# Attention layer: TensorE, VectorE and ScalarE run in a written order, probabilities are turned two units and multiplied four units behind their scores

## The chip, the cores and the metric

The kernel runs on one core of one Trainium2 chip. The metric is the device time of one execution in microseconds (us); a time that is reported is the median over runs. TensorE (PE) does matmuls and transposes, VectorE (DVE) and ScalarE (ACT) read and write PSUM and SBUF, GpSimd (POOL) works on SBUF, and SyncE (SP) issues most DMAs. Products that need fp32 accuracy are made of three single-pass products: each operand is split into a high part (rounded, `hi`) and a remainder (`lo`), and hi·hi + hi·lo + lo·hi is accumulated. In the code this is the loop over `PASS`.

## The reference, cut to what matters

A model of two layers works on 512 latent tokens and 256 context tokens of width 1024. Layer 0 is a gated DeltaNet and isn't touched. Layer 1 is attention with 8 query heads on 2 key/value heads of width 128, for the latent rows only:

```python
def gqa_attend(q, k, v):
    qg = q.reshape(b, lq, 2, 4, 128)
    s = jnp.einsum('bqhgd,bkhd->bhgqk', qg, k).astype(F32) * (d ** -0.5)
    p = jax.nn.softmax(s, axis=-1).astype(v.dtype)
    return jnp.einsum('bhgqk,bkhd->bqhgd', p, v).reshape(b, lq, hq, d)

# layer 1
u_lat, u_ctx = modulated_rms_norm(h_lat), modulated_rms_norm(h_ctx)
q, k, v, z = split(u @ w_in, [1024, 256, 256, 1024])   # q, k: RMS norm per head, then axial rotary
y_lat = (gqa_attend(q, concat(k_ctx, k_lat), concat(v_ctx, v_lat)) * silu(z)) @ w_out
out   = rms_norm(h_lat + gate * y_lat)
```

## The kernel before, in words

Line numbers are those of the kernel before, as in its profile. Layer 1 fills the last 334 us of the span, from about 985 us. The order in which each engine takes its instructions is set there by a scheduler that works when the program is built: it takes the program's order and a cost for each instruction, and puts independent work into gaps it sees. (Layer 0 has one loop, at L1045, whose order is written out by hand instead.) A buffer that is used again makes the new writer wait for the last user of the old contents.

**Inputs.** `u_block(k)` turns 128 columns of the residual stream into the transposed, modulated input `uL`: matmuls with a diagonal matrix into a PSUM bank (L1159), DVE scales and shifts it (L1161), ACT writes hi (L1162), DVE lo (L1163). `kv_block(k)` accumulates k and v (L1225). `kv_norm` takes sums of squares on ACT (L1233) and calls `rsqrt`. `k_tile(t)` rotates keys (L1256 and L1257 on DVE, an add on POOL, L1258) and `to_T` transposes them (PE L1264, ACT L1266 hi, DVE L1267 lo).

**Two shared PSUM banks.** `ptr` (L1069) is a pool of two PSUM banks with the tag `tr`. They are used in turn by `u_block`, by every `to_T`, by each half of every `turn`, and by `room` (L1088), which lends a bank as scratch to `rsqrt`. With `room`, `rsqrt` is a chain of 15 DVE operations on 128x8 (L163 to L172), most of them with one operand in PSUM; without it, 12 operations that have all operands in SBUF (L163, L164, L174 to L179).

**Units.** There are 32 units u: query head hq = u // 4, block of 128 rows t = u % 4. For a unit, `scores` makes 128x768 scores in `s3[:, u % 2]`: three matmuls on the 512 columns of the half's own bank (L1348), three on the 256 columns of the bank that both halves share (L1351). DVE takes the row maximum (L1353) and multiplies it by the query's norm factor r (L1355), ACT takes the exponential with its row sum (L1358), DVE the reciprocal (L1359), ACT scales the rows (L1360). `turn` transposes the 768 columns in two groups of three (PE L1373), each followed by ACT hi (L1375) and DVE lo (L1376). `values`, once per two units, does 18 matmuls into `po` (L1385); DVE multiplies by the gate z (L1387), ACT and POOL split the result (L1389, L1390).

**Pieces.** While units run, PE also projects z and q for the later heads. A `z_piece` is half of one head's z, 12 matmuls of 512 columns (L1335), with tanh (L1338) and a DVE product (L1339) behind the second half. A `q_piece` is 24 matmuls of 256 columns (L1319), two squares on ACT (L1322), the rotation on DVE (L1249 once, L1252 twice), an add on POOL (L1253), `to_T`, and behind t = 3 `rsqrt`. Eight units form a period that starts at u0 = 8p: z at u0 and u0+1, q for t = 0 to 3 at u0+2 to u0+5, z at u0+6 and u0+7. Each new q or z weight is cast and split on POOL (L1194, L1195). In the last period six `out_block` calls (6 matmuls of 512 columns each, L1404) take the place of pieces; the output weights are split on POOL (L1440, L1441).

The loop that says the program's order is short:

```python
    for u in range(32 + 3):
        if u < 32:
            scores(u)
        if u in pieces1:
            f_, x, y = pieces1[u]
            f_(x, y)
        if 0 <= u - 1 < 32:
            turn(u - 1)
        if u >= 3 and u % 2:
            values((u - 3) // 2)
```

Of the kernel before, what the change touches and what calls it, by code (L numbers as in the profile page):

```python
# [86 lines left out]
def backbone(tc, a, out):  # L87
# [1222 lines left out]
    def q_piece(p, t):  # L1310
# [4 lines left out]
        wq, sq = qTs["w", p], qTs["s", p]  # L1315
        pgq = pg[1 - t // 2].rearrange("p (t n) -> p t n", t=2)
        for k in range(KT):
            for n_, (i, j) in enumerate(PASS):
                T.matmul(pgq[:, t % 2], uL[i][:, k, t * P:(t + 1) * P], wq[j][:, k], start=k == 0 and n_ == 0, stop=k == KT - 1 and n_ == 2)  # L1319
        for h in range(2):  # L1320
            jk = tmp.tile([P, P], F32, tag="jk", name=f"qj{p}{t}{h}")
            S.activation(jk, pgq[:, t % 2, h * P:(h + 1) * P], AF.Square, accum_out=sq[:, t, h:h + 1])  # L1322
# [5 lines left out]
    def z_piece(hq, half):  # L1328
# [4 lines left out]
        for k in range(half * 4, half * 4 + 4):  # L1333
            for n_, (i, j) in enumerate(PASS):
                T.matmul(pg[b], wz[j][:, k], uL[i][:, k], start=k == 0 and n_ == 0, stop=k == KT - 1 and n_ == 2)  # L1335
        if half == 1:
            zt = at.tile([P, NLAT], F32, tag="zt", name=f"zt{hq}", bufs=3)
            S.activation(zt, pg[b], AF.Tanh, scale=0.5)  # L1338
            V.scalar_tensor_tensor(zt, zt, 1.0, pg[b], ALU.add, ALU.mult)  # L1339
            zts[hq] = zt  # L1340

    def scores(u):
# [3 lines left out]
        for n_, (i, j) in enumerate(PASS):  # L1346
            q = qTs[hq // 2][i][:, hq % 2, t * P:(t + 1) * P]
            T.matmul(s3[:, b, own], q, kT[j][:, g, own], start=n_ == 0, stop=n_ == 2)  # L1348
        for n_, (i, j) in enumerate(PASS):
            q = qTs[hq // 2][i][:, hq % 2, t * P:(t + 1) * P]  # L1350
            T.matmul(s3[:, b, shared], q, kT[j][:, g, shared], start=n_ == 0, stop=n_ == 2)  # L1351
# [1 line left out]
        V.tensor_reduce(nm_, s3[:, b], AX.X, ALU.max, negate=True)  # L1353
# [1 line left out]
        V.tensor_tensor(nm_, nm_, r, ALU.mult)  # L1355
# [2 lines left out]
        S.activation(pr, s3[:, b], AF.Exp, bias=nm_, scale=r, accum_out=sm)  # L1358
# [19 lines left out]
    def values(u2):  # L1378
# [4 lines left out]
        for kt_ in range(NT):  # L1383
            for n_, (i, j) in enumerate(PASS):
                T.matmul(po, vv[i][:, kt_, g * P:(g + 1) * P], pT[j][:, kt_], start=kt_ == 0 and n_ == 0, stop=kt_ == NT - 1 and n_ == 2)  # L1385
# [125 lines left out]
```

## Time and profile before

| | |
|---|---|
| runs | 1324.54 us median of 3 (1322.84, 1324.54, 1326.51) |
| profiled execution | span 1319.2 us from the first to the last instruction; the profile gives no other time of its own |
| busy over the span | PE 1182.4 us (90%), DVE 840.3 (64%), ACT 708.9 (54%), POOL 640.2 (49%) |
| chain of work that ended last | PE 51%, DVE 13%, POOL 11%, DMA 10%, ACT 9% |
| layer 1, from 985 us | PE 286.5 us busy of 334.2 |

A row of the timeline gives the start, the time until the end of the last of a run of equal instructions, engine, line, operation, output and inputs, and in brackets the idle time of the engine ahead of it and what ended it. A row of the table by windows gives start, end, length, then the busy time of PE, its weight loads, DVE, ACT and POOL, the granted clock of TensorE (1 is full speed), the share of the DMA engines and GB/s. A row of the groups gives busy time and the mean of one in ns. Starts of rows are 985 us and more because layer 0 comes first.

### The profile page before, as it was taken

To read this page: it belongs to the slowest core of one execution; us is meant where nothing else is said; L and a number is where in the kernel's file an instruction comes from. 1 tells how busy PE (TensorE), PEld (TensorE's weight loads), DVE (VectorE), ACT (ScalarE), POOL (GpSimd) and SP (SyncE) were. 2 spreads that over 40 slices of the span, in tenths; PEclk is the share of its full clock that TensorE was granted. 3 is DMA by queue.
4 is the path that set the end of the run, shared out by engine and by line. 5 is a ranking of instruction groups with operands and counts; after the bars stand their busy time and mean duration, and the time that the engine had idled before them with its cause. 6 is when DMAs were issued, how large, how long until landed. Compare 5 with 4: busy or idle time off the path is not lost.

```text
span 1319.2 us, 28137 instructions
## 1 busy us (share of the span) xinstructions
PE 1182.4 (90%) x10803; PEld 946.5 (72%) x10803; DVE 840.3 (64%) x1784; ACT 708.9 (54%) x1892; POOL 640.2 (49%) x503
## 2 busy tenths in 40 slices
PE   3999999998889798999988897897999879998886
PEld 1676778887778687886555565775777669887674
DVE  3688567768796456866767775654355567655635
ACT  3343336764666789856877774533332234565531
POOL 0121142079999998004754785575663144322520
PEclk9999999999899899999999999998999899998988
DMA  8367975464455796559999897544542021101113
GB/s 316 133 210 224 334 223 154 139 174 140 125 165 150 191 277 214 182 182 262 220 215 213 205 223 177 182 154 128 187 146 65 1 64 49 48 1 65 64 64 96
DMA packets 235304, 209.81 MB, mean 159 GB/s; under 512 B 51073, under 2 KB 195618, under 8 KB 234274
## 3 DMA queue, kind: packets, MB, share of 16 engines
q1 hardware_dynamic: 216354, 198.58, 52.2%
q10 hardware_dynamic: 18816, 9.44, 2.5%
q8 instruction: 85, 1.39, 0.5%
q14 instruction: 49, 0.40, 0.1%
HBM read 167.21 MB, written 40.67 MB: 158 GB/s over the span
## 4 chain that ended last, share of the span: by engine, by line
PE 51%; DVE 13%; POOL 11%; DMA 10%; ACT 9%; issue 4%; SPq 2%; ACTq 0%; DVEq 0%; POOLq 0%
PE ks L963 5%; PE g_q L324 5%; PE g_z L324 4%; PE po L1123 4%; DMA cT<-t_d 3%; POOL X L664 3%; PE pg L1319 3%; PE g_k L324 3%; PE kv L1225 3%; PE po L1385 3%; PE su L1019 3%; POOL tmp L663 2%; POOL wol L859 2%; PE pg L1335 2%; PE pr L989 2%
## 5 line engine op out<-in xcount | busy, mean ns | idle before, releaser
L972 POOL TENSOR_TENSOR S<-S,glb 128x512 f32<-128x512 f32 x88 | 89.9, 1042 | 128.4 <-DMA cv<-v_d 70.4
L1123 PE MATMUL po<-woh,y 128*128 128x512 f32 x384 | 128.1, 404 | 12.3 <-ACT y L887 9.1
L859 POOL TENSOR_TENSOR wol<-wo,woh 128x1024 fp32r<-128x1024 f32 x32 | 76.5, 2396 | 54.4 <-ACT woh L858 46.9
L324 PE MATMUL g_v<-uh,wh 128*128 128x512 f32 (+1 forms) x256 | 90.4, 353 | 11.6 <-DVE sil_v L350 11.6
L664 POOL TENSOR_TENSOR X<-X,tmp 128x62 f32<-128x62 f32 (+15 forms) x93 | 96.8, 1041 | 6.7
L963 PE MATMUL ks<-S,ckq 128*64 128x256 f32 x768 | 96.1, 392 | 0.6 <-ACT O L969 0.6
L324 PE MATMUL g_z<-uh,wh 128*128 128x512 f32 (+1 forms) x256 | 88.9, 347 | 7.8 <-DVE sil_v L350 7.8
L1123 PEld LDWEIGHTS po<-woh,y 128*128 128x128 f32 x384 | 71.9, 192 | 28.7 <-ACT y L887 9.8
L663 POOL TENSOR_TENSOR tmp<-L,X 128x62 f32<-128x62 f32 (+15 forms) x93 | 88.0, 946 | 6.7
L324 PE MATMUL g_v<-ul,wh 128*128 128x512 f32 (+1 forms) x256 | 89.3, 349 | 0.0
L324 PE MATMUL g_v<-uh,wl 128*128 128x512 f32 (+1 forms) x256 | 88.6, 346 | 0.0
L324 PE MATMUL g_z<-uh,wl 128*128 128x512 f32 (+1 forms) x256 | 87.4, 341 | 0.0
L324 PE MATMUL g_z<-ul,wh 128*128 128x512 f32 (+1 forms) x256 | 87.3, 341 | 0.0
L346 DVE SCALAR_TENSOR_TENSOR acc_v<-g_v,cwv,acc_v 128x510 f32<-128x510 f32 (+3 forms) x128 | 75.7, 610 | 17.4 <-ACT acc_v L343 15.4
L963 PEld LDWEIGHTS ks<-S,ckq 128*64 128x64 f32 x768 | 52.0, 139 | 41.9 <-ACT O L969 7.1
L1123 PE MATMUL po<-wol,y 128*128 128x512 f32 x192 | 78.5, 409 | 3.4 <-POOL wol L859 3.4
L306 POOL TENSOR_TENSOR wl_k<-w_k,wh_k 128x1024 fp32r<-128x1024 f32 x8 | 19.0, 2380 | 101.8 <-ACT wh_k L305 101.8
L324 PEld LDWEIGHTS g_v<-uh,wh 128*128 128x128 f32 x256 | 50.3, 196 | 18.1 <-DVE sil_v L350 12.1
L1037 DVE TENSOR_TENSOR S<-su,S 128x512 f32<-128x512 f32 x88 | 56.6, 685 | 7.2 <-PE su L1019 6.1
L966 DVE SCALAR_TENSOR_TENSOR r<-ks,negV,cv 128x128 f32<-128x128 f32 x192 | 56.4, 344 | 4.9 <-PE ks L963 3.8
L324 PEld LDWEIGHTS g_z<-uh,wh 128*128 128x128 f32 x256 | 49.3, 193 | 13.8 <-DVE sil_v L350 8.6
L1022 DVE TENSOR_TENSOR O<-pq,O 128x512 f32<-128x512 f32 x48 | 33.2, 691 | 40.5 <-PE pq L1011 35.3
(372 smaller groups left out, 3435.1 us busy)
## 6 DMA issues: line engine op xcount, KB each, us to landing
aw<-in_ada_w SPq DMA_DIRECT2D x24, 1024.0 KB, 7.7
w<-in_dn_w_in SPq DMA_DIRECT2D x40, 512.0 KB, 4.6
wo<-in_dn_w_out SPq DMA_DIRECT2D x32, 512.0 KB, 3.2
cv<-v_d SPq DMA_DIRECT2D x96, 128.0 KB, 3.5
df<-gc_d SPq DMA_DIRECT2D x48, 128.0 KB, 2.8
z_d<-zs SPq DMA_DIRECT2D x16, 384.0 KB, 4.7
v_d<-vt ACTq DMA_DIRECT2D x16, 384.0 KB, 4.4
t_d<-Tt SPq DMA_DIRECT2D x6, 1024.0 KB, 4.1
```

Source lines behind the costliest of these rows:

```text
L324: mm = T.matmul(pg_[:m, :n], w[:, k, :m], u[:, k, c0:c0 + n], start=k == 0 and n_ == 0, stop=k == KT - 1 and n_ == 2)
L346: V.scalar_tensor_tensor(acc[:, c0 + lo:c0 + hi], ps[:, lo + j - 2:hi + j - 2], cwv[:, j, ct:ct + 1], acc[:, c0 + lo:c0 + hi], ALU.mult, A ...
L663: E.tensor_tensor(tv, bcast(L[:, :, j + 1:, j], 3, j + 1), bcast(X[:, :, j, 0:j + 1], 2, n), ALU.mult)
L664: E.tensor_tensor(X[:, :, j + 1:, 0:j + 1], X[:, :, j + 1:, 0:j + 1], tv, ALU.subtract)
L859: G.tensor_tensor(wl, w, wh, ALU.subtract)
L963: T.matmul(ks[r0:r0 + 64, w], kq[:, hh, w, r0:r0 + 64], St[hh][:, d], start=True, stop=True)
L966: V.scalar_tensor_tensor(r[:, 2 * j + i], ks[:, 0, i], negV[:, visit, t, h:h + 1], v[:, h], ALU.mult, ALU.add)
L972: G.tensor_tensor(St[hh], St[hh], bcast(g_, 3, P), ALU.mult)
L1019: T.matmul(su[c0:c0 + 64, d ^ j, j], kt[r0:r0 + 64, hh, c0:c0 + 64], vd[r0:r0 + 64, 2 * j:2 * j + 2], start=True, stop=True)
L1037: V.tensor_tensor(St[hh], raw(sj, 0, [[512 - 1024 * j, 2], [P, 2], [1, P]]), St[hh], ALU.add)
L1123: T.matmul(acc[j][nh], y[i][:, j, :], ww[k][:, nh * 512:(nh + 1) * 512], start=h == 0 and x == 0, stop=h == VH - 1 and x == 2)
L1225: T.matmul(pkv[t], u_[i][:, k, c0:c0 + P], wkv[j][:, k], start=k == 0 and n_ == 0, stop=k == KT - 1 and n_ == 2)
```

## The change

Five things change, all in layer 1. Line numbers here are those of the changed kernel.

1. From just before the latent k/v loop to the end of the attention loop, PE, DVE and ACT take their instructions in the order in which the program writes them (`manual_schedule`). POOL and SP are still ordered by the scheduler. `u_block` is written one block ahead of `kv_block`, and the first q and z pieces, `kv_norm` and the k tiles are written interleaved.
2. A unit's work is written in another order: scores(u); `to_T` of the q piece of the iteration before; turn(u-2) in place of turn(u-1); the exponential of u; at even u, values of units u-4 and u-3 (before: at odd u, of u-3 and u-2); the scaling of u; then the piece of u, its matmuls and what follows them apart from `to_T`.
3. The row maximum is written to PSUM, into columns 256 to 263 of `po`'s bank (L1366), and its product with r goes from there to SBUF (L1369). `po` grows from 256 to 512 columns; `values` uses the first 256.
4. In a q piece the rotation stands ahead of the squares, and `rsqrt` for t = 3 takes a `tr` bank as scratch (L1334).
5. `out_block` starts at u = 27, so five blocks rather than six lie in the loop; the sixth moves to the final stage. The loop runs to 36.

```diff
     norms1((2, 3, 4, 5), "l")
+    manual = ExitStack()
+    manual.enter_context(tc.manual_schedule(engines={T.engine, V.engine, S.engine}))
+    u_block(0, 0, (2, 3, 4, 5), uL)
     for k in range(KT):
-        u_block(k, 0, (2, 3, 4, 5), uL)
+        if k + 1 < KT:
+            u_block(k + 1, 0, (2, 3, 4, 5), uL)
         kv_block(k, (2, 3, 4, 5))
...
+    def q_post(p, t, pgq):
+        sq = qTs["s", p]
+        qr = rotated(pgq.rearrange("p (h d) -> p h d", h=2), None, 0, t, f"q{p}{t}")
         for h in range(2):
             jk = tmp.tile([P, P], F32, tag="jk", name=f"qj{p}{t}{h}")
-            S.activation(jk, pgq[:, t % 2, h * P:(h + 1) * P], AF.Square, accum_out=sq[:, t, h:h + 1])
-        qr = rotated(pgq[:, t % 2].rearrange("p (h d) -> p h d", h=2), None, 0, t, f"q{p}{t}")
-        to_T(qr, qTs[p], 0, t * P, f"q{p}{t}")
+            S.activation(jk, pgq[:, h * P:(h + 1) * P], AF.Square, accum_out=sq[:, t, h:h + 1])
         if t == 3:
-            rsqrt(sq.rearrange("p t h -> p (t h)"), 1.0 / P)
+            sv = sq.rearrange("p t h -> p (t h)")
+            rsqrt(sv, 1.0 / P, room=room(f"q{p}", 8))
+        return qr
...
-        nm_ = at.tile([P, 1], F32, tag="nm", name=f"nm{u}")
+        small = po[:, 256 + 4 * b:260 + 4 * b]
+        nm_ = small[:, 0:1]
         V.tensor_reduce(nm_, s3[:, b], AX.X, ALU.max, negate=True)
+        nms = at.tile([P, 1], F32, tag="nm", name=f"nm{u}", bufs=3)
         r = qTs["s", hq // 2][:, t, hq % 2:hq % 2 + 1]
-        V.tensor_tensor(nm_, nm_, r, ALU.mult)
+        V.tensor_tensor(nms, nm_, r, ALU.mult)
...
-    po = pS.tile([P, 256], F32, tag="po", name="po1")
-    for u in range(32 + 3):
+    po = pS.tile([P, 512], F32, tag="po", name="po1")
+    late_q = []
+    for u in range(32 + 4):
         if u < 32:
             scores(u)
+        for f_ in late_q:
+            f_()
+        late_q = []
+        if 0 <= u - 2 < 32:
+            turn(u - 2)
+        if u < 32:
+            exps(u)
+        if u >= 4 and u % 2 == 0:
+            values((u - 4) // 2)
+        if u < 32:
+            scaled(u)
         if u in pieces1:
-            f_, x, y = pieces1[u]
-            f_(x, y)
-        if 0 <= u - 1 < 32:
-            turn(u - 1)
-        if u >= 3 and u % 2:
-            values((u - 3) // 2)
+            main, post, x, y = pieces1[u]
+            z_ = post(x, y, main(x, y))
+            if main is q_main:
+                late_q.append(lambda z_=z_, x=x, y=y: to_T(z_, qTs[x], 0, y * P, f"q{x}{y}"))
...
-        if 26 <= u < 32:
-            out_block(u - 26, 0, pg)
+        if 27 <= u < 32:
+            out_block(u - 27, 0, pg)
+    manual.close()
```

Two places show how this moves instructions. The first is PE around the last q piece of the second period (q for t = 3, in unit 13): `s3` are scores, `qtq23` the transposes of that piece (p = 2, t = 3), `po1` values, `pt12` the turn of unit 12. Before:

```order
L1351 MATMUL s3_12446<-kT0_11759,qT1_0_12547 128x256
L1351 MATMUL s3_12446<-kT1_11760,qT1_0_12547 128x256
L1351 MATMUL s3_12446<-kT0_11759,qT1_1_12548 128x256
L1385 MATMUL po1_12447<-pT5_0_13207,vv0_11761 128x256
L1264 MATMUL qtq23_13356<-ident_60,qrq23_13350 128x128 x2
L1385 MATMUL po1_12447<-pT5_1_13208,vv0_11761 128x256
L1385 MATMUL po1_12447<-pT5_0_13207,vv1_11762 128x256
```

After:

```order
L1323 MATMUL pg0_12142<-wq2_0_13100,uL1_11771 128x256
L1363 MATMUL s3_12452<-kT0_11759,qT1_0_12553 128x512
L1363 MATMUL s3_12452<-kT1_11760,qT1_0_12553 128x512
L1363 MATMUL s3_12452<-kT0_11759,qT1_1_12554 128x512
L1363 MATMUL s3_12452<-kT0_11759,qT1_0_12553 128x256
L1363 MATMUL s3_12452<-kT1_11760,qT1_0_12553 128x256
L1363 MATMUL s3_12452<-kT0_11759,qT1_1_12554 128x256
L1264 MATMUL qtq23_13393<-ident_60,qrq23_13356 128x128 x2
L1395 MATMUL pt12_0_13400<-ident_60,pr12_13240 128x128 x3
L1395 MATMUL pt12_1_13406<-ident_60,pr12_13240 128x128 x3
L1407 MATMUL po1_12453<-pT5_0_13226,vv0_11761 128x256
```

The transposes of the q piece now stand between six score matmuls and both groups of the turn, with only the scores between them and the piece's last projection (pg0); before, the values of two units lay around them and the turn of unit 12 further on.

The second place is DVE behind the same piece: `qrq23` and `tmq23` are the rotation, `sq2`, `rs` and `roomq2` the rsqrt, `nm` the row maximum and its product, `pT` the lo parts of a turn, `ay` the gate product. Before:

```order
L163 TENSOR_SCALAR sq2_13102<-sq2_13102 128x8
L164 TENSOR_SCALAR rs0_20_13361<-sq2_13102 128x8
L1353 TENSOR_REDUCE nm11_13160<-s3_12446 128x1
L174 TENSOR_SCALAR rs0_20_13361<-rs0_20_13361 128x8
L1249 TENSOR_TENSOR qrq23_13350<-pg0_12140,cg0_11763 128x256
L1252 TENSOR_TENSOR tmq23_13351<-pg0_12140,sg0_11765 128x2x64 x2
L1267 TENSOR_TENSOR qT2_1_13101<-qtq21_13202,qT2_0_13100 128x2x128
L1355 TENSOR_TENSOR nm11_13160<-nm11_13160,sq1_12549 128x1
L177 SCALAR_TENSOR_TENSOR rs1_20_13362<-rs0_20_13361 128x8
L1376 TENSOR_TENSOR pT5_1_13208<-pt10_0_13209,pT5_0_13207 128x3x128
L178 TENSOR_TENSOR rs1_20_13362<-rs1_20_13362,sq2_13102 128x8
L1387 SCALAR_TENSOR_TENSOR ay4_13239<-po1_12447,zt2_12928 128x256
```

After (the first of the rsqrt's operations and the rotation stand ahead of these rows):

```order
L169 COPY rs0_20_13367<-roomq2_13366 128x8
L170 SCALAR_TENSOR_TENSOR roomq2_13366<-roomq2_13366,rs0_20_13367 128x8
L171 TENSOR_TENSOR roomq2_13366<-roomq2_13366,sq2_13112 128x8
L172 SCALAR_TENSOR_TENSOR sq2_13112<-roomq2_13366,rs0_20_13367 128x8
L1366 TENSOR_REDUCE po1_12453<-s3_12452 128x1
L1369 TENSOR_TENSOR nm14_13391<-po1_12453,sq1_12555 128x1
L1267 TENSOR_TENSOR qT2_1_13111<-qtq23_13393,qT2_0_13110 128x2x128
L1398 TENSOR_TENSOR pT6_1_13399<-pt12_0_13400,pT6_0_13398 128x3x128
L1398 TENSOR_TENSOR pT6_1_13399<-pt12_1_13406,pT6_0_13398 128x3x128
L1378 RECIPROCAL sm14_13413<-sm14_13413 128x1
L1409 SCALAR_TENSOR_TENSOR ay5_13434<-po1_12453,zt2_12938 128x256
```

Where the rsqrt was spread between a maximum, a rotation and the lo parts, it now stands in one piece ahead of the maximum of unit 14, the lo part of `to_T` and both lo parts of the turn.

More of the change, by code (lines that the diff above doesn't have):

```diff
@@ L1335, in z_piece, with z_post @@
                 T.matmul(pg[b], wz[j][:, k], uL[i][:, k], start=k == 0 and n_ == 0, stop=k == KT - 1 and n_ == 2)
+        return pg[b]
+    def z_post(hq, half, pz):
         if half == 1:
             zt = at.tile([P, NLAT], F32, tag="zt", name=f"zt{hq}", bufs=3)
[L1338 to L1339 removed]
+            S.activation(zt, pz, AF.Tanh, scale=0.5)
+            V.scalar_tensor_tensor(zt, zt, 1.0, pz, ALU.add, ALU.mult)
             zts[hq] = zt
+    sms = {}
     def scores(u):
@@ L1345, in scores, with exps, scaled @@
         own, shared = (slice(0, 512), slice(512, 768)) if b == 0 else (slice(256, 768), slice(0, 256))
[L1346 to L1351, printed above, removed]
-        nm_ = at.tile([P, 1], F32, tag="nm", name=f"nm{u}")
+        for c in (own, shared):
+            for n_, (i, j) in enumerate(PASS):
+                q = qTs[hq // 2][i][:, hq % 2, t * P:(t + 1) * P]
+                T.matmul(s3[:, b, c], q, kT[j][:, g, c], start=n_ == 0, stop=n_ == 2)
+        small = po[:, 256 + 4 * b:260 + 4 * b]
+        nm_ = small[:, 0:1]
         V.tensor_reduce(nm_, s3[:, b], AX.X, ALU.max, negate=True)
+        nms = at.tile([P, 1], F32, tag="nm", name=f"nm{u}", bufs=3)
         r = qTs["s", hq // 2][:, t, hq % 2:hq % 2 + 1]
-        V.tensor_tensor(nm_, nm_, r, ALU.mult)
+        V.tensor_tensor(nms, nm_, r, ALU.mult)
+        sms[u] = nms, r
+    def exps(u):
+        b = u % 2
+        nms, r = sms[u]
         pr = at.tile([P, NTOK], F32, tag="pr", name=f"pr{u}", bufs=3)
-        sm = at.tile([P, 1], F32, tag="sm", name=f"sm{u}")
-        S.activation(pr, s3[:, b], AF.Exp, bias=nm_, scale=r, accum_out=sm)
+        sm = at.tile([P, 1], F32, tag="sm", name=f"sm{u}", bufs=3)
+        S.activation(pr, s3[:, b], AF.Exp, bias=nms, scale=r, accum_out=sm)
         V.reciprocal(sm, sm)
+        prs[u] = pr, sm
+    def scaled(u):
+        pr, sm = prs[u]
         S.activation(pr, pr, AF.Copy, scale=sm)
-        prs[u] = pr
     def turn(u):
@@ L1384, in values @@
             for n_, (i, j) in enumerate(PASS):
-                T.matmul(po, vv[i][:, kt_, g * P:(g + 1) * P], pT[j][:, kt_], start=kt_ == 0 and n_ == 0, stop=kt_ == NT - 1 and n_ == 2)
+                T.matmul(po[:, 0:256], vv[i][:, kt_, g * P:(g + 1) * P], pT[j][:, kt_], start=kt_ == 0 and n_ == 0, stop=kt_ == NT - 1 and n_ == 2)
         y32 = at.tile([P, 256], F32, tag="y32", name=f"ay{u2}", bufs=1)
-        V.scalar_tensor_tensor(y32, po, 0.5, zts[hq][:, c0:c0 + 256], ALU.mult, ALU.mult)
+        V.scalar_tensor_tensor(y32, po[:, 0:256], 0.5, zts[hq][:, c0:c0 + 256], ALU.mult, ALU.mult)
         ys = [y[:, hq, c0:c0 + 256] for y in yT]
@@ L1404, in out_block @@
                 T.matmul(acc[nh], yT[i][:, k, t * P:(t + 1) * P], wo[j][:, k, nh * 512:(nh + 1) * 512], start=k == 0 and n_ == 0, stop=k == KT - 1 and n_ == 2)
-    z_piece(0, 0)
-    z_piece(0, 1)
-    q_piece(0, 0)
+    z_main(0, 0)
     kv_norm((2, 3, 4, 5), "l")
+    z_post(0, 1, z_main(0, 1))
+    qr = {}
+    turned = lambda t: to_T(qr.pop(t), qTs[0], 0, t * P, f"q0{t}")
+    x = q_main(0, 0)
     k_tile(2)
+    qr[0] = q_post(0, 0, x)
+    x = q_main(0, 1)
     k_tile(3)
-    q_piece(0, 1)
+    turned(0)
+    qr[1] = q_post(0, 1, x)
+    x = q_main(0, 2)
     k_tile(4)
+    turned(1)
+    qr[2] = q_post(0, 2, x)
+    x = q_main(0, 3)
     k_tile(5)
-    for t in (2, 3):
-        q_piece(0, t)
+    turned(2)
+    qr[3] = q_post(0, 3, x)
+    turned(3)
     psG_c.__exit__(None, None, None)
@@ L1462, in backbone @@
             if t < 3:
-                for k in range(6 if t == 0 else 0, KT):
+                for k in range(5 if t == 0 else 0, KT):
                     out_block(k, t, acc[t])
```

19 lines of the change are left out of this document (10 added, 9 removed).

## The prediction

> **What bounds the kernel now.** I read the windows of layer 1 first, cut where units start: the projections (985 to 1049 us), units 0 to 7, units 8 to 23, the last units, the final stage. Layer 0, before 985 us, is the same in both kernels and stays out of the sum.
>
> ```profile
> 985.00:1049.00 64.00, 55.53 (x308) 46.06 (x307) 33.12 (x106) 17.00 (x66) 17.16 (x14) 0.97 0.16 53
> 1049.00:1117.50 68.50, 60.04 (x382) 53.75 (x382) 43.91 (x94) 27.97 (x72) 31.07 (x24) 0.96 0.17 50
> 1117.50:1221.00 103.50, 95.54 (x624) 85.50 (x623) 65.63 (x152) 57.67 (x133) 35.80 (x31) 0.97 0.12 39
> 1221.00:1271.20 50.20, 39.51 (x221) 33.26 (x221) 28.09 (x47) 26.18 (x47) 22.06 (x16) 0.92 0.16 53
> 1271.20:1319.20 48.00, 35.84 (x154) 28.63 (x152) 22.64 (x73) 5.91 (x17) 0.73 (x1) 0.89 0.33 99
> ```
>
> PE is the nearest bound: 95.5 of 103.5 us in the middle. So what can be won there is 8 us of idle time and whatever PE loses at a lower clock, and what can be lost is open. The chain from 1000 us, by line, and the waits from 985 us say what interrupts PE:
>
> ```profile
> by line: PE pg L1319 11.9%; PE po L1385 10.5%; PE pg L1335 9.6%; PE s L1348 7.3%; PE pso L1404 6.8%; PE kv L1225 6.4%; PE pt L1373 3.9%; ACT pr L1358 3.7%; DVE nm L1355 3.6%; PE s L1351 3.4%; DVE nm L1353 3.3%; PE pso L1470 2.9%; issue 2.6%
> ACT pr L1358 <- DVE nm L1355: 38.8, 20, 9.5
> PE s L1348 <- ACT pr L1358: 15.1, 8, 3.3
> L1355 DVE TENSOR_TENSOR nm<-nm,sq 128x1 f32<-128x1 f32 x32 | 22.8, 712 | 0.4
> ```
>
> The exponential waits for the product of the maximum and r (38.8 us), and the next scores wait for the exponential (15.1 us in 8 places). That product is one column and takes 712 ns in the mean. The timeline has the scores of units 0, 1, 2, 8, one unit between, and 24; the starts are my marks:
>
> ```profile
> 1049.06 1.63 PE L1348 MATMUL s<-kT,qT 128*128 128x512 f32 x3
> 1065.73 1.65 PE L1348 MATMUL s<-kT,qT 128*128 128x512 f32 x3 [3.26 <-ACT pr L1358]
> 1072.53 0.86 PE L1348 MATMUL s<-kT,qT 128*128 128x512 f32 x3
> 1117.53 0.87 PE L1348 MATMUL s<-kT,qT 128*128 128x512 f32 x3
> 1210.41 1.65 PE L1348 MATMUL s<-kT,qT 128*128 128x512 f32 x3 [2.76 <-ACT pr L1358]
> 1221.06 0.86 PE L1348 MATMUL s<-kT,qT 128*128 128x512 f32 x3
> ```
>
> A period of eight units takes (1221.06 - 1117.53)/2 = 51.8 us; the first two units take 23.5. Behind idle times of 2.76 and 3.26 us the same three matmuls take 1.65 rather than .86: PE runs at half speed for a while.
>
> **The price of each step.** Starts of successive rows give PE's prices, since ends overlap:
>
> ```profile
> 1123.41 0.86 PE L1348 MATMUL s<-kT,qT 128*128 128x512 f32 x3
> 1124.11 0.52 PE L1351 MATMUL s<-kT,qT 128*128 128x256 f32 x3
> 1111.68 0.82 PE L1373 MATMUL pt<-ident,pr 128*128 128x128 f32 x6
> 1133.29 0.38 PE L1264 MATMUL qtq<-ident,qrq 128*128 128x128 f32 x2
> 1099.27 4.82 PE L1335 MATMUL pg<-uL,wz 128*128 128x512 f32 x20 [0.47 <-ACT qT L1266]
> 1112.25 3.23 PE L1319 MATMUL pg<-wq,uL 128*128 128x256 f32 x25
> 1116.49 1.20 PE L1385 MATMUL po<-pT,vv 128*128 128x256 f32 x8
> ```
>
> With some .15 us of drain at each end taken off: scores .70 + .37 = 1.07, turn .66, `to_T` .24, half a z 12 x .235 = 2.81, a q piece 24 x .1235 = 2.96, values 18 x .1195 = 2.15. A period holds 8 scores and turns, 4 values, 4 z halves, 4 q pieces with `to_T`: 13.8 + 8.6 + 11.2 + 12.8 = 46.5 us. Before, 5.3 us of a period are loss. The change keeps this work, so its worth is the loss that the written order leaves. For that I step through a period with these prices of the others:
>
> ```profile
> 1125.69 0.95 DVE L1353 TENSOR_REDUCE nm<-s 128x1 f32<-128x768 f32 x1
> 1126.67 0.16 DVE L1355 TENSOR_TENSOR nm<-nm,sq 128x1 f32<-128x1 f32 x1
> 1126.87 0.99 ACT L1358 ACTIVATE pr<-s,nm,sq 128x768 f32<-128x768 f32 x1 [0.28 <-DVE nm L1355]
> 1117.32 0.42 DVE L1249 TENSOR_TENSOR qrq<-pg,cg 128x256 f32<-128x256 f32 x1 [0.49 <-ACT qj L1322]
> 1117.67 0.48 DVE L1252 TENSOR_TENSOR tmq<-pg,sg 128x128 f32<-128x128 f32 x2
> 1118.22 0.75 POOL L1253 TENSOR_TENSOR qrq<-qrq,tmq 128x256 f32<-128x256 f32 x1 [2.73 <-DVE tmq L1252]
> 1109.68 0.36 ACT L1266 CAST qT<-qtq 128x256 fp32r<-128x256 f32 x1
> 1110.07 0.42 DVE L1267 TENSOR_TENSOR qT<-qtq,qT 128x256 fp32r<-128x256 f32 x1
> 1118.52 1.02 DVE L1376 TENSOR_TENSOR pT<-pt,pT 128x384 fp32r<-128x384 f32 x2 [0.38 <-ACT pT L1375]
> L1338 ACT ACTIVATE zt<-pg 128x512 f32<-128x512 f32 x8 | 4.8, 597 | 5.2 <-PE pg L1335 5.1
> ```
>
> Times below count from the start of a unit's scores.
>
> *What is won.* The exponential of u is awaited only by scores(u+1), the turn uses a unit two back, values four back: the 15.1 us of waits for L1358 have 3 to 6 us of cover in every unit. The maximum goes through PSUM. What an operand there is worth shows in the rsqrt rows, of one shape class:
>
> ```profile
> L178 DVE TENSOR_TENSOR rs<-rs,sq 128x8 f32<-128x8 f32 x12 | 8.1, 671 | 0.4
> L170 DVE SCALAR_TENSOR_TENSOR roomkc<-roomkc,rs 128x4 f32<-128x4 f32 x3 | 0.5, 170 | 0.1
> 1100.48 4.75 POOL L1195 TENSOR_TENSOR wq<-w1q,wq 128x1024 fp32r<-128x1024 f32 x2
> 1100.76 2.14 DVE L164 TENSOR_SCALAR rs<-sq 128x8 int32<-128x8 int32 x1
> ```
>
> All in SBUF: 671 ns in the mean, and 2.14 us while POOL works on two SBUF tiles; one operand in PSUM: 170 ns. So L1369 should cost .16 each time. The Trainium skill (SBUF — State Buffer, "SBUF: two separate sides") has a DVE operation with two SBUF inputs and a GpSimd operation that reads SBUF exclude each other for a whole instruction; the 671 against 170 ns agree.
>
> *Values at even u* write `po`, whose bank now also holds the maximum, so they wait for L1369 of their own unit. At u0 and u0+2 DVE first has the gate product behind a tanh of .60 us, so the maximum runs from 1.65 to 2.61 and L1369 to 2.77; PE is there at 1.73. Loss 1.04 twice. u0 lasts 2.77 + 2.15 + 2.81 = 7.73, u0+2 7.88, the z units u0+1 and u0+7 1.07 + .66 + 2.81 = 4.54.
>
> *The late `to_T`* in u0+3 to u0+6 stands right behind the scores. The rotation of .83 starts when the projection ends, the add of .75 follows: ready at about 1.76, PE there at 1.07, loss .7. It takes one of two `tr` banks, the turn's first group the other, and the second group waits until DVE has made the lo part, which stands behind the maximum (2.6): at 3.07, loss .67. u0+3 and u0+5 last 3.40 + 2.96 = 6.36, u0+4 with values 8.51.
>
> *The rsqrt* ahead of u0+6 is 15 DVE operations of .2 each, 3.0 us, in one piece; the maximum, both lo parts and the turn's bank (room holds one) queue behind it. Two of its operations, L163 and L164, are in SBUF throughout, and POOL now gets its casts for the next weight:
>
> ```profile
> 1097.80 2.02 POOL L1194 CAST wq<-w1q 128x1024 fp32r<-128x1024 f32 x2
> 1099.78 0.74 POOL L1253 TENSOR_TENSOR qrq<-qrq,tmq 128x256 f32<-128x256 f32 x1
> ```
>
> The add is again behind two casts, so `to_T` runs at 2.9 rather than 1.76; L164 is locked until about 3.0, the room is free at 5.6, the maximum ends at 6.55, L1369 at 6.76, the second group goes at 7.3, values at 7.6, z at 9.75, end at 12.55. PE idles 1.85, 2.4 and 1.3 us here; as the 2.76 us of the row at 1210.41 brought half speed, I add 1.5 (0 to 2.8): 14.0. Without lock and slow clock it is 11.5. The Trainium skill (TensorE: Matmul & The Clock Gate, "Why this matters for your kernels") asks only that no idle gap exceeds about 3 us, by which the 1.5 would fall away in all three periods, 4.5 us less; 2.76 us sufficed here, so the row decides.
>
> Sum of a period: 7.73 + 4.54 + 7.88 + 6.36 + 8.51 + 6.36 + 14.0 + 4.54 = **59.9 us**, against 51.8.
>
> **The sum.** Against the span of 1319.2, by marks.
>
> *A, to the scores of unit 2.* The written projections have ten `to_T` each behind its rotation with less between. Estimated PE waits: 2.75 for the first k tile (15 rsqrt operations of .17 ahead of it), .65 to 1.0 for four others, 2.85 for the last q (nothing left to put between), 1.2 at both ends of the latent loop, 10.4 in all, 5 more than now, so unit 0 starts near 1054. Units 0 and 1 then take 13 rather than 23.5, as nothing but the rsqrt of q0 delays the first exponential. -5.3 (-10 to +2).
>
> *B, unit 2 to 8:* 59.9 - 7.73 - 4.54 - 3.1 (unit 2 has no values yet) = 44.5 against 45.0: -0.5 (-5 to +3).
>
> *C, unit 8 to 24:* 2 x 59.9 = 119.8 against 103.5: **+16.3** (+8 to +22).
>
> *D, unit 24 to the end:*
>
> ```profile
> 1206.87 4.67 POOL L1441 TENSOR_TENSOR wo<-wf,wo 128x1024 fp32r<-128x1024 f32 x2
> 1281.35 22.66 PE L1404 MATMUL pso<-wo,yT 128*128 128x512 f32 x96
> ```
>
> Units 24 and 25 take 12.3, 26 to 31 29.8 (with about 6 of waits for output weights and for L1369), then 43.5 of PE (27 out blocks of 6 matmuls at 22.66/96 = .236 make 38.2, the last two values and turns the rest), and 11.5 for what follows the last matmul: 97.1 against 98.1. -1.0 (-8 to +4); the sixth out block only moves.
>
> Total +9.5: span 1328.7. The median of the runs lies 5.3 above the profiled span, so **1334 us**.
>
> **The rivals.** B holds most of one period and C two, so for a period of E us the time is about 1334 + 3 x (E - 59.9).
>
> *The stalls are milder, no change* (chance .18). L164 isn't locked and the clock stays up (11.5 for 14.0), and .25 of each of the three add waits is covered: E = 59.9 - 2.5 - .7 = 56.7, time 1324. For it: the prices are means, and the row at 1100.76 caught POOL's second kind of operation, not a cast. Against: the row at 1210.41.
>
> *Faster: the locks were the loss* (.26). L1355's excess is 32 x (.712 - .16) = 17.7 us, and its 3.6% of the chain's 320 us, 11.5, lie on the chain. If DVE without these locks runs ahead of PE all through, the values' wait (2.1) and the bank waits (2.0) go too, the rsqrt is unlocked (2.5), and its queue is shorter by the gain in the maximum (1.3): E = 52.0, time 1310. It decides below E = 55.4 (4 us under the median), when the stalls of a period are 8.9 rather than 13.4. For it: PE's 5.3 us of loss in a period are partly these. Against: the waits for POOL's add and for the room come from orders that no faster DVE operation changes.
>
> *Much slower* (.04): PE stays at half speed behind each gap of 1.8 us, E = 65, time 1349.
>
> **How the numbers follow.** Forecast .52, stalls milder .18, faster .26, much slower .04. A change of less than .3%, 4 us, can't be told from none here: faster .26, same .18, slower .56. The forecast alone spans 1328.5 to 1348 (E from 58 to 64.5). The range goes down to 1310, since the milder stalls and the upper half of the faster case have to lie in it: .13 is left out below, .04 above.
>
> **What would show it.** In the changed profile: L1369 at .16 each; scores no longer waiting for the exponential; transposes of `to_T` waiting .7 for POOL's add, the turn's second group for DVE's `to_T` lo; in each u0+6 an idle PE of 5 us behind the rsqrt, the scores of u0+7 near 14 after it; L164 of 2 us under POOL. Units 8 to 24 near 120 us carry the forecast: near 113 makes it the rival without change, 104 the faster one. The forecast is wrong if the unit 2 mark moves by far more than 5 us, or if the waits named appear with other engines' work under them.

## The result and the profile after

| kernel | median us | ratio to the kernel before, 95% interval |
|---|---|---|
| before (beside the changed one) | 1323.69 | 1 |
| changed | 1342.91 (1340.53 to 1346.47) | 1.0142 [1.0114, 1.0171] |

The change makes the kernel 19 us slower; 10 were forecast. The first question is where. The rows below are the marks of the prediction in the timeline of the changed kernel: the first large group of `u_block` matmuls of the latent rows, then the scores of units 0, 2, 8 and 24. Scores now appear as groups of six matmuls.

```profile
1002.09 1.95 PE L1159 MATMUL ht<-dn,h 128*128 128x128 f32 x16
1070.00 1.30 PE L1363 MATMUL s<-kT,qT 128*128 128x512 f32 x6
1081.34 1.21 PE L1363 MATMUL s<-kT,qT 128*128 128x512 f32 x6
1126.95 1.22 PE L1363 MATMUL s<-kT,qT 128*128 128x512 f32 x6
1247.36 1.23 PE L1363 MATMUL s<-kT,qT 128*128 128x512 f32 x6
```

The first of these groups started at 993.71 in the kernel before:

```profile
993.71 1.95 PE L1159 MATMUL ht<-dn,h 128*128 128x128 f32 x16
```

| stretch | before | changed | difference | forecast |
|---|---|---|---|---|
| to the latent `u_block` | 993.7 | 1002.1 | +8.4 | 0 |
| from there to unit 0 | 55.4 | 67.9 | +12.6 | +5 |
| unit 0 to unit 2 | 23.5 | 11.3 | -12.1 | -10.5 |
| unit 2 to 8 (B) | 45.0 | 45.6 | +0.6 | -0.5 |
| unit 8 to 24 (C) | 103.5 | 120.4 | +16.9 | +16.3 |
| unit 24 to the end (D) | 98.1 | 97.3 | -0.8 | -1.0 |

The second and third rows are A, which the prediction gives as -5.3 in all.

The 8.4 us of the first row lie in layer 0, which all kernels here share. In the profiled executions of the eleven other kernels below and above that mark lies between 990.8 and 1003.9, and two kernels of the same projections stand near both ends (990.8 in run 8, 1003.6 in run 10). So it differs between profiled executions and says nothing of the change; what moves it isn't settled. From that mark on the changed kernel takes 342.6 us rather than 325.5: +17.1, near the 19.2 of the medians. Below, "layer 1" is this length, from the mark to the end of the span.

What PE waited for in layer 1 of the changed kernel, from the waits (us in total, times, longest):

```profile
PE qtq L1264 <- POOL qrq L1253: 13.5, 13, 2.7
PE pt L1395 <- DVE qT L1267: 7.5, 12, 0.8
PE pt L1395 <- DVE sq L172: 7.0, 3, 2.5
PE po L1407 <- DVE nm L1369: 5.8, 8, 0.8
PE pg L1323 <- DVE qrk L1256: 4.8, 2, 2.5
PE s L1363 <- ACT pr L1377: 3.7, 2, 3.4
```

The wait that the change was to remove, scores for the exponential, is down from 15.1 us in 8 places to 3.7 in 2: 3.4 in unit 1 and .3 in unit 30. In its place stand four others, 33.8 us: late transposes for POOL's add, the turn for the lo part of `to_T`, the turn for the rsqrt (L172 is its last operation), values for the product of the maximum.

Unit 14 (u0+6 of the second period) shows three of them one behind the other. From its timeline, between the scores of units 14 and 15:

```profile
1168.61 1.22 PE L1363 MATMUL s<-kT,qT 128*128 128x512 f32 x6
1168.84 2.03 POOL L1194 CAST wq<-w1q 128x1024 fp32r<-128x1024 f32 x2 [4.91 <-PE pg L1323]
1170.82 0.72 POOL L1253 TENSOR_TENSOR qrq<-qrq,tmq 128x256 f32<-128x256 f32 x1
1170.92 0.65 DVE L164 TENSOR_SCALAR rs<-sq 128x8 int32<-128x8 int32 x1
1171.60 0.44 PE L1264 MATMUL qtq<-ident,qrq 128*128 128x128 f32 x2 [1.78 <-POOL qrq L1253]
1174.08 0.17 DVE L172 SCALAR_TENSOR_TENSOR sq<-roomq,rs 128x8 f32<-128x8 f32 x1
1174.16 0.96 DVE L1366 TENSOR_REDUCE po<-s 128x1 f32<-128x768 f32 x1
1174.30 0.59 PE L1395 MATMUL pt<-ident,pr 128*128 128x128 f32 x3 [2.26 <-DVE sq L172]
1175.70 0.90 PE L1395 MATMUL pt<-ident,pr 128*128 128x128 f32 x3 [0.81 <-DVE qT L1267]
1176.25 4.19 PE L1407 MATMUL po<-pT,vv 128*128 128x256 f32 x18
1183.57 1.22 PE L1363 MATMUL s<-kT,qT 128*128 128x512 f32 x6
```

The add stands behind two casts on POOL, the maximum behind the whole rsqrt on DVE, the first group of the turn behind the rsqrt's bank, the second behind the lo part that follows the maximum. Then 18 value matmuls take 4.19 us, at a granted clock of .50; they take 2.4 in unit 12, which has no such stops. The unit lasts 14.96 us.

### The profile page after: what moved, and what is told of

Read it like the earlier page. It is cut to its first block, busy times and chain, and to the rows that moved or that the text cites. A ratio compares the mean times of both kernels' runs of the same rounds, so it can differ in the third digit from the quotient of the medians.

```text
span 1344.7 us, 28136 instructions
## 1 busy us (share of the span) xinstructions
PE 1191.8 (89%) x10803; PEld 951.6 (71%) x10803; DVE 816.1 (61%) x1796; ACT 711.7 (53%) x1892; POOL 639.9 (48%) x503
## 4 chain that ended last, share of the span: by engine, by line
PE 46%; DVE 12%; POOL 12%; DMA 12%; ACT 10%; issue 4%; SPq 3%; ACTq 0%; DVEq 0%; POOLq 0%
PE ks L963 5%; PE g_z L324 4%; PE po L1123 4%; PE g_q L324 4%; PE pg L1323 3%; PE po L1407 3%; PE g_k L324 3%; POOL X L664 3%; DMA cT<-t_d 3%; POOL wol L859 2%; POOL tmp L663 2%; PE su L1019 2%; PE pg L1344 2%; PE kv L1225 2%; PE pr L989 2%
## 5 line engine op out<-in xcount | busy, mean ns | idle before, releaser
L859 POOL TENSOR_TENSOR wol<-wo,woh 128x1024 fp32r<-128x1024 f32 x32 | 76.3, 2390 | 55.4 <-ACT woh L858 55.3
L324 PE MATMUL g_v<-uh,wh 128*128 128x512 f32 (+1 forms) x256 | 90.2, 352 | 12.1 <-DVE sil_v L350 12.1
```

Source lines behind the costliest of these rows:

```text
L324: mm = T.matmul(pg_[:m, :n], w[:, k, :m], u[:, k, c0:c0 + n], start=k == 0 and n_ == 0, stop=k == KT - 1 and n_ == 2)
L859: G.tensor_tensor(wl, w, wh, ALU.subtract)
```

## The experiments

Runs 1 to 4 change one thing in the changed kernel, run 5 one thing in the kernel before. Runs 6 and 8 change several things together; runs 7, 9 and 10 start from one of these two.

**1. The rsqrt behind the values.**

```diff
+        norm_q()          # rsqrt(sq, room=...) of a q piece with t == 3
         if u < 32:
             scaled(u)
```

> One edit to the changed kernel: the rsqrt of a q piece's t = 3 is written behind the values of u0+6 rather than ahead of that unit's maximum. Theory (the long DVE piece holds the maximum, the lo parts and the turn's bank): u0+6 falls from a mean of 14.3 us (14.7, 15.0, 13.2) to about 9.5, since only the wait for POOL's add behind two casts is left; three times 4.7, the kernel 14 us faster than the changed one (about 1329). Rival (POOL's casts hold the unit, the rsqrt only fills a wait that is there anyway): u0+6 stays above 12, the gain is under 6 us.

Measured: 1326.01 us, ratio 1.0015 [0.9997, 1.0033]; layer 1 330.3. Against the changed kernel's ratio that is 17 us, by layer 1 of the profiles 12.3. The unit u0+6 of the three periods lasts 9.7, 11.1 and 8.7 us rather than 14.7, 15.0 and 13.2, which is 13.3 us in all. In unit 14 the maximum now stands right behind the scores, the transposes wait 1.77 for POOL as before, and no other long wait is left; the values still run slowly at first (in unit 6, behind stops of the same lengths, they take 2.41):

```profile
1157.92 0.97 DVE L1372 TENSOR_REDUCE po<-s 128x1 f32<-128x768 f32 x1 [0.17 <-PE s L1369]
1159.66 0.44 PE L1264 MATMUL qtq<-ident,qrq 128*128 128x128 f32 x2 [1.77 <-POOL qrq L1253]
1161.02 0.90 PE L1401 MATMUL pt<-ident,pr 128*128 128x128 f32 x3 [0.59 <-DVE qT L1267]
1161.57 3.63 PE L1413 MATMUL po<-pT,vv 128*128 128x256 f32 x18
```

The place of the rsqrt accounts for most of what the change lost, and the rival that only POOL's casts hold the unit falls.

**2. `to_T` behind the next piece's matmuls.**

```diff
-        for f_ in late_q:
-            f_()
...
+            z_ = main(x, y)
+            for f_ in late_q:
+                f_()
+            z_ = post(x, y, z_)
```

> One edit to the changed kernel: to_T of a q piece is written behind the projection matmuls of the next unit's piece rather than behind its scores. Theory (PE waits for POOL's add and then for the tr bank, .7 + .6 us in u0+3 to u0+5): those three units fall to about 5.1, 7.2 and 5.2 us, and u0+6 by 1 to 2, as the second group of its turn no longer waits for the lo part of to_T; 3 x (3 x 1.35 + 1.5) = 17 us at most, 12 to 15 expected, about 1329. Rival (the bank wait only changes hands, since both banks are held until DVE's lo parts, which stand behind the maximum): the add's .7 goes, the bank's .6 stays, 6 us.

Measured: 1333.38, ratio 1.0072 [1.0046, 1.0098], some 9 us faster than the changed kernel by the ratios, 7 by layer 1 (335.4). The add and bank waits are gone (u0+3 4.9 us, u0+5 5.7), but 12 to 15 were expected. In u0+4 only .4 is won, as the values of that even unit now reach their wait for the maximum, and in u0+6 nothing: it lasts 15.4, 15.1 and 13.8 us. There the whole stall now stands at the rsqrt:

```profile
PE pt L1395 <- DVE sq L172: 16.2, 3, 6.1
PE po L1407 <- DVE nm L1369: 9.3, 14, 1.0
```

In these two units, removing the first wait handed its time to the next one.

**3. The maximum back in SBUF.**

```diff
-        small = po[:, 256 + 4 * b:260 + 4 * b]
-        nm_ = small[:, 0:1]
+        nm_ = at.tile([P, 1], F32, tag="nmx", name=f"nmx{u}", bufs=3)
```

> One edit to the changed kernel: the row maximum is written to SBUF again, so po's bank is touched by values alone. Theory (in this order the exponential has several us of cover, so a slower product costs nothing on PE, while values no longer wait for it): u0 and u0+2 fall by .8 to 1.0 each, 6 us in all, less where the lo parts queue behind a slowed product in units under POOL's splits: 2 to 6 us faster than the changed kernel. Rival (the wait of the one-column product for POOL is what counts): the product goes back to a mean near .7 us and the kernel is 8 us or more slower than the changed one.

Measured: 1340.36, ratio 1.0127 [1.009, 1.0164]; layer 1 341.0 against 342.6. The interval overlaps the changed kernel's, so a gain of 2 us isn't shown by the times. The timeline shows both sides: u0 and u0+2 last 6.61 and 6.72 rather than 7.63 and 7.77, just the 1.04 of the wait of values, and the product is slow again:

```profile
L1368 DVE TENSOR_TENSOR nm<-nmx,sq 128x1 f32<-128x1 f32 x32 | 17.2, 539 | 1.1
```

The changed kernel has 158 ns there. In the written order of the change that costs PE little: units 8 to 24 take 116.4 us rather than 120.4, and the other stretches give 2.4 of that back.

**4. The projections by the scheduler, the loop as in the change.**

```diff
-    manual.enter_context(tc.manual_schedule(engines={T.engine, V.engine, S.engine}))   # ahead of the latent k/v loop
...
+    manual.enter_context(tc.manual_schedule(engines={T.engine, V.engine, S.engine}))   # ahead of the unit loop
     for u in range(32 + 4):
```

> The written order begins only at the attention loop: the projections ahead of it are in the order of the kernel before, and are ordered by the scheduler. Theory (the written projections stop PE six times, 10.7 us, and some 6 us more go to half speed behind these stops; but the scheduler filled part of its own stops with the first two units, which it can't here): unit 0 starts 5 to 9 us earlier after the first latent u_block than the 67.9 us of the changed kernel, 7 us faster in all. Rival (all of the excess over the 55.4 us before comes from the order of the projections): 12 us earlier.

Measured: 1336.61, ratio 1.0107 [1.0072, 1.0141]; layer 1 340.2. Unit 0 starts 55.2 us behind the mark rather than 67.9, but units 0 and 1 take 19.2 rather than 11.3: together 74.4 for 79.3, 4.9 us. (The two intervals overlap; by the ratios the gain is 4.6.) The rival's 12 us are there up to unit 0 and are mostly given back. By the rows that is q and k work that isn't done by then: 24 q matmuls stand between the two score groups of unit 0, PE waits 1.37 us for the squares of that piece and 2.15 for the first exponential, and the granted clock of the two units is .79.

**5. The maximum in PSUM alone, in the kernel before.**

```diff
+        small = po[:, 256 + 4 * b:260 + 4 * b]
+        nm_ = small[:, 0:1]
...
-    po = pS.tile([P, 256], F32, tag="po", name="po1")
+    po = pS.tile([P, 512], F32, tag="po", name="po1")
```

> The kernel before with one part of the change alone: the row maximum goes to PSUM beside the values, its product with r from there to SBUF; all orders are the scheduler's. If the product's waits for POOL were the loss of the kernel before (the rival of the prediction that had it faster), the mean of the product falls from .71 to .16 us and the time by most of the 11.5 us that it holds of the chain, 8 us or more. Theory now (what bounds is the order in which PE meets its waits): the product falls to .16, the wait of the exponential for it shrinks, but values now wait for the maximum in the same bank and other DVE operations still wait for POOL; 2 to 6 us faster.

Measured: 1319.53 against 1324.83, ratio 0.996 [0.9938, 0.9982]. The group of the product and two of the waits:

```profile
L1357 DVE TENSOR_TENSOR nm<-po,sq 128x1 f32<-128x1 f32 x32 | 4.8, 151 | 0.4
ACT pr L1360 <- DVE nm L1357: 27.4, 23, 8.7
PE po L1387 <- DVE nm L1357: 4.6, 6, 0.9
```

The product falls from 712 to 151 ns, 18 us less DVE time, and the kernel gains 5 us. The exponential still waits for the product, now because DVE comes late to the maximum or, with other work in between, to its product; values pay 4.6 us for the shared bank. This part of the change is a gain in itself; the larger size that the faster rival gave it is not borne out.

**6. The loop in another order.** One unit now reads:

```diff
         if 0 <= u - 2 < 32:
             turn(u - 2)
         if u < 32:
             exps(u)
+            scaled(u)
+        if u % 8 == 7 and u < 24:
+            norm_q(u // 8 + 1)            # rsqrt, all in SBUF
+        piece = pieces1.get(u)
+        if piece:
+            z_ = piece[0](*piece[2:])     # the piece's matmuls
+        for f_ in late_q:                 # to_T of the last q piece
+            f_()
...
         if u >= 4 and u % 2 == 0:
             values((u - 4) // 2)
+        if piece:
+            z_ = post(x, y, z_)
```

> The changed kernel with the attention loop written in another order, nothing else: in a unit scores, turn, exponential, scaling, then the piece's matmuls, then to_T of the last q piece, then values (or an output block and values), then what follows the piece; the rsqrt a unit later (u0+7, behind the reciprocal) and without a tr bank, except for q0. All three waits of the period then have 2.8 to 3 us of matmuls ahead of them. Theory (the period's loss is these three waits and the slow clock behind them): u0 6.7, u0+1 4.5, u0+2 6.9, u0+3 5.0, u0+4 7.1, u0+5 5.3, u0+6 7.0, u0+7 4.5, a period of 47 us instead of 59.9, 35 us over units 2 to 24, about 1308. Rival (behind them stands another bound, POOL's splits or DVE, so a new wait appears): a period above 51, 1320 or more.

Measured: 1303.13 against 1324.83, ratio 0.9848 [0.9803, 0.9892]. Units 8 to 24 take 97.0 us, 48.5 a period, by windows from the scores of unit 8 to those of unit 24 (columns as before: PE, weight loads, DVE, ACT, POOL busy, then the granted clock):

```profile
1106.30:1203.31 97.01, 92.91 (x641) 85.07 (x640) 59.78 (x149) 57.48 (x133) 31.95 (x28) 1.00 0.11 33
```

The changed kernel's answer for the same stretch:

```profile
1126.95:1247.36 120.41, 100.53 (x641) 89.25 (x640) 58.04 (x154) 58.51 (x133) 31.95 (x28) 0.96 0.09 27
```

The same 641 matmul records and nearly the same work on the others, 23 us less; and PE itself is 7.6 us less busy, at a granted clock of 1.00 rather than .96. So the stops cost twice here, as idle time and as slow matmuls behind them. What is left above the 47 expected is one wait in u0, behind the rsqrt of the unit before:

```profile
1160.90 2.42 PE L1407 MATMUL po<-pT,vv 128*128 128x256 f32 x18 [1.47 <-DVE nm L1369]
```

**7. That loop, with the projections by the scheduler.** The edit of run 4 on top of run 6, with one more difference: the rsqrt of the first q (q0) takes no `tr` bank.

> The loop of the run above, and the projections ahead of it by the scheduler. If the parts add up: 5 us faster than the loop alone, as it was with the loop of the change (74.4 rather than 79.3 us from the first latent u_block to unit 2), about 1303. If the scheduler's end of the projections leaves unit 0 waiting for more: no gain.

Measured: 1302.63, ratio 0.9827 [0.978, 0.9874]: no gain that can be told from run 6. Marks: from the first latent group to unit 2 78.6 us, 78.1 in run 6. That is 4.2 us more than in run 4. What differs by the rows is the first rsqrt, which lies all in SBUF here and runs while POOL subtracts; no run tests it alone:

```profile
1059.61 0.67 DVE L164 TENSOR_SCALAR rs<-sq 128x8 int32<-128x8 int32 x1
1060.31 2.32 DVE L174 TENSOR_SCALAR rs<-rs 128x8 int32<-128x8 int32 x1
1062.65 2.26 DVE L177 SCALAR_TENSOR_TENSOR rs<-rs 128x8 f32<-128x8 f32 x1
1064.95 0.17 DVE L178 TENSOR_TENSOR rs<-rs,sq 128x8 f32<-128x8 f32 x1
1067.94 2.29 PE L1359 MATMUL s<-kT,qT 128*128 128x512 f32 x6 [5.72 <-ACT pr L1373]
```

Unit 1 waits 5.72 us for the first exponential; in run 4, with a PSUM bank as scratch, the operations behind L164 took .17 each and unit 1 waited 2.15.

**8. That loop, with the projections written in another order.**

```diff
+    x0 = q_main(0, 0)
+    k2 = k_turned(2)                  # rotation only
+    q0 = q_post(0, 0, x0)
+    x2 = q_main(0, 2)                 # the other PSUM bank
+    k3 = k_turned(3)
+    kT_(k2, 2)
+    qT_(q0, 0)
+    q2 = q_post(0, 2, x2)
+    x1 = q_main(0, 1)
...
+    pieces1 = {u - 1: x for u, x in pieces1.items()}
+    del pieces1[-1]
+    pieces1[0] = (z_both, z_post, 1, 1)
```

> The loop of the second run, and the projections written so that two q pieces in succession use different PSUM banks (t = 0, 2, 1, 3), each rotation stands ahead of the projection that covers it, the context k tiles a block or two later, four rotation buffers, and both halves of the second z in unit 0, with all later pieces a unit earlier. Theory (the stops of the written projections come from their order, and the slow clock from the stops): the first latent u_block to unit 0 takes 57 to 59 us rather than 67.9, of which unit 0 gives 3 back; 6 to 9 us faster than the loop alone, about 1300. Rival (rotation and POOL's add are too slow for any order): no more than the 5 us of the scheduler.

Measured: 1293.06, ratio 0.9768 [0.9723, 0.9813], 10 us faster than run 6 by the medians and 7.1 by layer 1; the intervals just overlap. Its first rsqrt is all in SBUF as well. Unit 0 starts 54.2 us behind the mark, unit 2 72.0 (run 6: 78.1), and it has one q piece more behind it by then. Units 8 to 24:

```profile
1096.49:1190.33 93.84, 92.64 (x641) 85.22 (x640) 55.21 (x149) 57.53 (x132) 28.52 (x26) 1.00 0.11 35
```

46.9 us a period: the 46.5 that the prediction summed from PE's prices alone. PE is idle 1.2 us in 93.8.

**9. Run 8 with the maximum in SBUF.** The edit of run 3.

> The fastest version so far (both loop and projections reordered, ratio to the kernel before .977), with the row maximum in SBUF rather than PSUM. Values stand behind 2.8 us of matmuls there, so nothing is won by freeing po's bank; the product of the maximum falls back to a mean of .5 us or more under POOL's splits. Theory (the product has cover in this order too): within .3% of the version with PSUM. Rival (its waits for POOL delay DVE's lo parts and with them the turns): slower by 4 us or more.

Measured: 1304.75 against 1325.81, ratio 0.9848 [0.9815, 0.988], slower than run 8 by .8%, some 10 us by these ratios, 4.2 by layer 1 of the profiles (303.1 and 298.9). My theory fell: the next scores wait for the exponential for 13.3 us in 8 places, 8.3 in 4 in run 8. Cover for it is thin in the short z units once PE doesn't stop elsewhere. From the timeline of unit 9:

```profile
1112.52 2.40 POOL L1195 TENSOR_TENSOR wz<-w1z,wz 128x1024 fp32r<-128x1024 f32 x1
1113.87 1.07 DVE L1372 TENSOR_TENSOR nm<-nmx,sq 128x1 f32<-128x1 f32 x1
1114.98 0.99 ACT L1380 ACTIVATE pr<-s,nm,sq 128x768 f32<-128x768 f32 x1 [1.92 <-DVE nm L1372]
1116.11 1.32 PE L1367 MATMUL s<-kT,qT 128*128 128x512 f32 x6 [0.76 <-ACT pr L1380]
```

The product ends as POOL's split ends, the exponential follows, and the next scores wait. The same part was worth nothing measurable in the order of the change (run 3).

**10. Run 8 with the depths of the kernel before.**

```diff
-        if 0 <= u - 2 < 32:
-            turn(u - 2)
+        if 0 <= u - 1 < 32:
+            turn(u - 1)
...
-        if u >= 4 and u % 2 == 0:
-            values((u - 4) // 2)
+        if u >= 3 and u % 2:
+            values((u - 3) // 2)
```

> The same fastest version with the depths of the kernel before: turn(u-1), and at odd u values of u-3 and u-2. Theory (what counts is that the exponential and the scaling stand ahead of the piece's matmuls, so a unit's probabilities are ready before the next unit's scores end, at about 4.9 us of at least 4.5 + 1.07): turn never waits for the scaling by more than a few tenths, time within .4% of the version with two and four. Rival (the depth is what takes the exponential off the path): PE waits for the scaling in the short z units, .5 us or more in each of 32 units, 15 us slower.

Measured: 1291.47, ratio 0.9728 [0.9688, 0.9768]. Its interval overlaps that of run 8, so no gain of two and four units over one and two is shown here. If there is a difference, it goes the other way: 5 us by the ratios, 6.9 by layer 1 (292.0 for 298.9). In units 8 to 24 run 10 takes 1.5 us more than run 8 (95.3 for 93.8). From unit 24 to the end it takes 90.2 for 99.4; some 2.8 of these are one turn and one set of values less to do there, and run 8 stops for 2.72 us in unit 26, at a granted clock of .50 behind it. No wait of PE for the scaling is left; its three largest waits in layer 1:

```profile
PE s L1367 <- ACT pr L1381: 5.2, 4, 2.9
PE po L1411 <- DVE nm L1373: 3.7, 3, 1.5
PE qtk L1264 <- POOL qrk L1258: 2.4, 1, 2.4
```

This version is 2.7% faster than the kernel before and 4% faster than the changed one.

## Why the prediction was right, and where it was not

**The period (B, C): right, step by step.** 59.9 us were forecast for eight units; the second period took 61.1, the third 59.3. By unit from u0, forecast and second period: 7.73 and 7.63, 4.54 and 4.45, 7.88 and 7.77, 6.36 and 6.49, 8.51 and 8.65, 6.36 and 6.67, 14.0 and 14.96, 4.54 and 4.48. The wait of values for the product, 1.04 twice a period, is shown by its removal in run 3. The add and bank waits of `to_T` are shown by run 2, with the same .7 and .6. The rsqrt's place is shown by run 1: 14 us were expected of it, 13.3 came in the three units and 17 in the medians. One price did not come out of the row shown with it: the start of the next row there gives 18 values 2.3 us, not 2.15; run 8's rows bear out the 2.15 (18 from 1194.90 to the scores at 1197.06).

**The lock in u0+6: right in the end, not in the way.** I had L164 locked by the casts until 3.0 us into the unit. It took .65 there, under a cast of 1.0, and the chain was as late as forecast because the rsqrt started later: DVE waited .75 us for the squares on ACT, which I had not priced. Under POOL's subtraction L164 does take 2.3 us (2.26 in run 2).

**The slow clock in u0+6: a term in the right place.** 1.5 us were added (0 to 2.8). In unit 14 the value matmuls alone lost 1.8 and z .6. That a stop of this length brings the low clock was open even in the kernel before: behind 3.09 us of idle time, longer than the 2.76 that the prediction took as its sign, PE kept full speed there (granted clock 1.00 over the next 3 us).

```profile
1244.27 0.97 PE L1348 MATMUL s<-kT,qT 128*128 128x512 f32 x3 [3.09 <-ACT pr L1358]
```

**A, the stretch up to unit 2: the step that failed.** -5.3 was forecast, +0.4 measured from the first latent `u_block` on. The stops of the written projections add up as forecast, 10.4 us against 10.7 in six, but in part by luck. The two large terms came nearly as priced, the first k tile (2.75 forecast, 2.09 measured) and the last q (2.85 and 2.66). Of the four other `to_T` at .65 to 1.0 only two waited, .45 and .69; and two stops of q projections, 2.37 and 2.47, were not in the sum at all. The profile names DVE for the two, but each ends .06 us after the last square on ACT of the q piece before, which lies in the other half of the same PSUM bank; in run 8, where successive pieces use different banks, neither is there. "5 more than now" was too much as well: PE waits 7.1 us in the same stretch before, so it is 3.

Of the 12.6 us that unit 0 comes later, 4.1 are idle time of PE. Some 4 are 31 matmuls that the kernel before does only behind the start of unit 0 (302 for 271 records; an estimate from the prices), and units 0 and 1 are shorter by them. The rest is what the prediction left out: it gave only units in the loop the half speed that can follow a stop. From the timeline of the projections and unit 1:

```profile
1021.23 0.73 PE L1264 MATMUL qtk<-ident,kr 128*128 128x128 f32 x2 [2.09 <-DVE kr L1274]
1021.76 1.92 PE L1159 MATMUL ht<-dn,h 128*128 128x128 f32 x8
1023.33 3.58 PE L1225 MATMUL kv<-wkv,uL 128*128 128x512 f32 x12
1042.92 3.03 PE L1323 MATMUL pg<-wq,uL 128*128 128x256 f32 x24
1049.20 5.49 PE L1323 MATMUL pg<-wq,uL 128*128 128x256 f32 x24 [2.37 <-DVE qrk L1256]
1062.13 4.58 PE L1323 MATMUL pg<-wq,uL 128*128 128x256 f32 x24 [2.47 <-DVE qrk L1256]
1069.80 0.44 PE L1264 MATMUL qtq<-ident,qrq 128*128 128x128 f32 x2 [2.66 <-POOL qrq L1253]
1071.13 2.91 PE L1344 MATMUL pg<-uL,wz 128*128 128x512 f32 x12
1077.43 1.32 PE L1363 MATMUL s<-kT,qT 128*128 128x512 f32 x6 [3.39 <-ACT pr L1377]
```

24 projection matmuls take 3.03 us, but 5.49 and 4.58 behind idle times of 2.37 and 2.47; with the group behind the 2.09 that is 5.6 us, the size of the whole difference in A. The two longest stops, 2.66 and 3.39 us, were not followed by slow matmuls. Run 8 agrees from the other side: the stretch to unit 0 falls by 13.7 us, 7.2 of it idle time of PE and 6.5 busy time at nearly the same work (300 matmul records for 302, granted clock 1.00 for .90).

The prediction named one sign of being wrong for A, a mark of unit 2 that moves by far more than 5 us. It moved by 8.8, of which 8.4 are the shift of layer 0, so the sign as it was put says little.

**D** was -1.0 and came at -0.8. The range of 1310 to 1348 held the time; the total of +9.5 was half of the 19.2 measured. Of the missing 9.7, 5.7 are A and 1.9 the other stretches; the last 2 lie between the layer 1 of two profiled executions and the medians.

**The rivals.** The milder stalls (56.7 a period) and the faster case (52.0) did not occur in this order, nor did a period of 65. The faster rival's mechanism is real but was sized wrongly: the maximum in PSUM gives 5 us alone (run 5), not most of 11.5. In an order in which PE meets almost none of the new waits (runs 8 and 9) it is worth 4 to 10 us. And the slow order was not the price of a written order: with the same means and another sequence the kernel is faster than both (runs 6, 8 and 10).

## What to carry to other kernels

When an order is written out by hand, walk one period with the measured durations and ask of each PE instruction what it waits for on the other engines: here that walk gave every unit of the second period within 1 us, and the cure of each stall was to put the longest independent group of matmuls between a result and its use, and the long chain of small operations (the rsqrt) where nothing queues behind it. Price a stop of PE together with the matmuls behind it, and as a range: in the projections three stops of 2.1 to 2.5 us cost 1.5 to 2.5 us more each, two longer ones nothing. Test the parts of a change in the final order too: the PSUM maximum was worth nothing that the times show in one order and 4 to 10 us in another, and for the depth of the pipeline, the most visible part, no gain is shown in the good one.
